# A float32 decoder trunk on one core: bucket transfers in three groups, two tables loaded later, the latents' norm moved into the query's projection

## The chip, the cores and the metric

One NeuronCore of a Trainium2 chip runs the whole program. The metric is the device time of one execution in microseconds. A core has a matrix engine (TensorE, in rows PE), VectorE (DVE), ScalarE (ACT), GpSimd (POOL) and SyncE (SP), which issues nearly all of the DMA transfers here. Each engine runs its own list of instructions in the order of the program and waits on semaphores for the others.

## The reference

A decoder trunk of two layers on 256 tokens of width 1024, all in float32. The first layer has differential attention with a bucketed relative bias; then one shared latent key and value is made; the second layer has multi-head latent attention. Cut to what matters here:

```python
def diff_attention(h, pos, w_qkv, ...):
    qkv = h @ w_qkv
    ...
    bucket = t5_bucket(p_blk[:, :, None] - pos[:, None, :])
    bias = jnp.take(rel_table, bucket, axis=0)
    sc = jnp.where(causal_mask(i, s), sc + bias, NEG_INF)
    a = jax.nn.softmax(sc, axis=-1)
    wts = a[:, :, 0] - lam * a[:, :, 1]
    ...

def shared_latent_kv(h, pos, kv_norm, w_dkv, ...):
    ckv_full = rms_norm(h, kv_norm) @ w_dkv
    c_kv = rms_norm(ckv_full[..., :256], ckv_norm)
    k_pe = rotary(rms_norm(ckv_full[..., 256:], k_pe_norm), pos)
    kv = c_kv @ w_ukv
    ...

def mla_attention(h, pos, w_dq, cq_norm, w_uq, ...):
    c_q = rms_norm(h @ w_dq, cq_norm)
    q = c_q @ w_uq
    ...
```

After each attention come a gated FFN with a causal convolution and a gated per-layer embedding, each with its residual.

## The kernel before, in words

**Weights** come as units of 128 x 1024 words (512 KB), in the order of use. `fetch` (L221 to L230) takes the next of five `st` buffers and has SP issue the transfer. `split_unit` (L235 to L243) makes two halves for a product in three matmuls: ScalarE casts a rounded high part `wh` (L242), and VectorE or GpSimd subtracts it for the low part `wl` (L243, here "lo-split"). Which of the two does it is set by `share`: the fraction of units that goes to GpSimd. `mm3` (L196 to L201) then issues high x high, low x high and high x low; a matmul of 128 columns by 256 is one of these.

**Order.** `weave` and `later` interleave streams as the code is run: attention heads with projections, and a step that is put off by so many units of PE work (`LAG`). A list scheduler then fills each engine's list, by its own estimate of what is ready and in the order of the code otherwise; inside `tc.high_priority()` it prefers an instruction, and `tc.issue_after(x)` keeps one behind instruction x. So the order that comes out is read from the lists (below), not from the code alone. PSUM banks lie in small pools (A 3, T 1, B 2, C 2), so a matmul that takes a bank over waits for the last reader of the old tile.

**First layer.** `proj_a(p)` projects query, key and value of two heads each; `post` squares, norms and transposes them (ACT L341, DVE L342 to L352, GpSimd's power L276 and PE's transposes L193). `bias_prep` (L384 to L437), between the projections, computes the bucket of each distance and writes the 128 x 384 table to device memory (L425, L426). `bias_loads` (L439 to L450) reads it back, broadcast to 32 partitions a piece: 24 transfers of 128 KB into six tiles `oh`. It is put off by `later(LAG, ...)` and issues all 24 at once. `bias_mm` (L452 to L474) compares each tile with the partition's index (DVE L457), does 96 small matmuls for each of three groups with a table of bias values in three parts (PE L464), and has ScalarE write the bias out (L470). Units 12 to 15 are the weights that the projections need next. Attention begins with L529.

**Constants.** `cst` holds gains and small tables; its last part, for the convolution, is loaded after `proj_a` has been queued (L684), and `grow`, two gain rows for the latents, at L862. Both stand in SP's list between the first weight units.

**Between the layers.** With `share` at 0.75 the latent `lps` is projected (320 columns), then `tok_mean` (L301 to L305) sums the squares of the residual by a small matmul with ones (L303), `lat_post` (L985 to L1019) makes the latents' norm and its rotary part (L990 to L1003), and then the query's latent is projected into `dps` (matmuls of 512 columns). `lat_T` transposes the normed latents (PE L193) behind the last of these. `cq_post` norms the query's latent. Then `share` is 0.3, and `fl_b` (L1180) walks `B_ORDER`, a list of items (keys and values, rotary, queries, output projections), woven with the heads of `attn_b`.

## Time and profile before

| what | value |
|---|---|
| median of 3 runs | 789.13 us (787.8 to 789.29) |
| profiled execution | 791.89 us |
| its span | 790.1 us |
| PE busy | 759.5 us, 96%, 6396 matmuls |
| VectorE busy | 560.9 us, 71% |
| ScalarE busy | 486.6 us, 62% |
| GpSimd busy | 278.9 us, 35% |
| mean granted clock of PE | 0.985 |
| read from device memory | 125.75 MB, 161 GB/s over the span |

The profile is of one execution. Its span runs from the first to the last instruction, and 1.8 us of the execution's time lie around it. An engine's busy time is the time in which one of its instructions runs; where an instruction starts late, the row names how long the engine sat idle before it and what released it. [...] Matmuls overlap, so the time of one is read from start to start.

### The profile page before, as it was taken

What the parts mean: (1) busy time and instruction counts of PE and PEld (TensorE: products, weight loads), DVE (VectorE), ACT (ScalarE), POOL (GpSimd) and SP (SyncE); (2) the same over time, 40 slices, a digit from 0 to 9 for tenths busy, and PEclk for the clock granted to TensorE, in tenths of its full rate; (3) what the DMA queues carried; (4) which work ended last, traced back from release to release, by engine and by line L of the source; (5) the groups of instructions that cost most, each with busy time, mean ns of one, the idle gap of its engine ahead of it and who ended that gap; (6) DMA issues with size and microseconds to landing.
All of it is one profiled execution on the core that took longest, in us unless ns stands there. A gap on an engine that the chain in (4) does not pass through costs nothing.

```text
span 790.1 us, 16494 instructions
## 1 busy us (share of the span) xinstructions
PE 759.5 (96%) x6396; PEld 746.0 (94%) x6396; DVE 560.9 (71%) x1137; ACT 486.6 (62%) x1044; POOL 278.9 (35%) x191
## 2 busy tenths in 40 slices
PE   7969999999999999999988999999999999999996
PEld 6969999999999999999978899999999999999996
DVE  6573888658997786546568878866568877875544
ACT  6535887667666665447856777554666666655442
POOL 2653365143233411116735463431333233201221
PEclk9988999999999999999999899999999999999999
DMA  8882345355656576555345132344455556665531
GB/s 317 256 263 92 115 143 166 83 175 154 204 183 185 173 250 207 183 172 172 111 145 183 35 114 71 116 131 130 135 189 172 185 178 186 190 185 186 188 107 54
DMA packets 37519, 127.97 MB, mean 162 GB/s; under 512 B 4672, under 2 KB 6208, under 8 KB 37440
## 3 DMA queue, kind: packets, MB, share of 16 engines
q1 hardware_dynamic: 36720, 126.38, 51.0%
q8 instruction: 50, 0.82, 0.4%
q10 hardware_dynamic: 720, 0.53, 0.2%
q14 instruction: 29, 0.24, 0.1%
HBM read 125.75 MB, written 1.15 MB: 161 GB/s over the span
## 4 chain that ended last, share of the span: by engine, by line
PE 83%; DVE 6%; DMA 3%; ACT 3%; issue 2%; POOL 1%; SPq 1%; DVEq 0%; ACTq 0%; POOLq 0%
PE pa L199 17%; PE pa L201 17%; PE pa L200 17%; PE pc L201 8%; PE pc L200 8%; PE pc L199 8%; DMA st<-in_wall 2%; DVE wl L243 1%; PE pb L529 1%; PE pb L199 1%; PE pt L193 1%; DMA oh<-s 1%; ACT wh L242 1%; POOL wl L243 1%; PE pb L200 1%
## 5 line engine op out<-in xcount | busy, mean ns | idle before, releaser
L242 ACT CAST wh<-st 128x1024 fp32r<-128x1024 f32 x221 | 230.6, 1050 | 171.7 <-PE pa L200 59.1
L243 DVE TENSOR_TENSOR wl<-st,wh 128x1024 fp32r<-128x1024 f32 x156 | 197.9, 1271 | 99.5 <-ACT wh L242 98.3
L243 POOL TENSOR_TENSOR wl<-st,wh 128x1024 fp32r<-128x1024 f32 x65 | 159.8, 2459 | 236.6 <-ACT wh L242 226.7
L201 PE MATMUL pa<-hgH,wl 128*128 128x256 f32 x496 | 141.1, 284 | 0.4 <-POOL wl L243 0.4
L200 PE MATMUL pa<-hgL,wh 128*128 128x256 f32 x496 | 140.5, 283 | 0.0
L199 PE MATMUL pa<-hgH,wh 128*128 128x256 f32 x496 | 140.1, 283 | 0.0
L199 PE MATMUL pa<-wh,hgH 128*128 128x256 f32 x328 | 95.2, 296 | 8.7 <-ACT bias L470 6.0
L199 PE MATMUL pa<-og,wh 128*128 128x256 f32 x352 | 99.9, 287 | 1.4 <-DVE hT L615 1.4
L200 PE MATMUL pa<-og,wh 128*128 128x256 f32 x352 | 99.4, 284 | 0.0
L201 PE MATMUL pa<-og,wl 128*128 128x256 f32 x352 | 99.4, 283 | 0.0
L199 PE MATMUL pc<-hgH,wh 128*128 128x256 f32 x336 | 95.1, 284 | 2.0 <-DVE pa L776 1.4
L201 PE MATMUL pc<-hgH,wl 128*128 128x256 f32 x336 | 95.2, 284 | 1.3 <-DVE wl L243 1.3
L200 PE MATMUL pa<-wl,hgH 128*128 128x256 f32 x328 | 95.0, 291 | 1.5 <-DVE wl L243 0.8
L200 PE MATMUL pc<-hgL,wh 128*128 128x256 f32 x336 | 95.4, 284 | 0.5 <-DVE hgL L209 0.5
L201 PEld LDWEIGHTS pa<-hgH,wl 128*128 128x128 f32 x496 | 95.2, 192 | 0.7 <-POOL wl L243 0.6
L200 PEld LDWEIGHTS pa<-hgL,wh 128*128 128x128 f32 x496 | 95.2, 192 | 0.0
L199 PEld LDWEIGHTS pa<-hgH,wh 128*128 128x128 f32 x496 | 95.1, 192 | 0.1
L201 PE MATMUL pa<-wh,hgL 128*128 128x256 f32 x328 | 94.2, 289 | 0.3 <-DVE hgL L206 0.3
L298 POOL TENSOR_TENSOR ssq<-ssq,d 128x256 f32<-128x256 f32 x35 | 35.9, 1027 | 158.5 <-ACT d L297 158.0
L199 PEld LDWEIGHTS pa<-wh,hgH 128*128 128x128 f32 x328 | 63.8, 197 | 10.9 <-ACT qk L208 6.1
L199 PEld LDWEIGHTS pa<-og,wh 128*128 128x128 f32 x352 | 66.9, 191 | 1.8 <-DVE hT L615 1.6
L200 PEld LDWEIGHTS pa<-og,wh 128*128 128x128 f32 x352 | 67.3, 191 | 0.3
(304 smaller groups left out, 1915.2 us busy)
## 6 DMA issues: line engine op xcount, KB each, us to landing
st<-in_wall SPq DMA_DIRECT2D x225, 512.0 KB, 3.6
oh<-s SPq DMA_DIRECT2D x24, 128.0 KB, 4.0
hT<-in_x SPq DMA_DIRECT2D x4, 256.0 KB, 5.6
st<-in_wall SPq DMA_DIRECT2D x4, 256.0 KB, 5.7
st<-in_xn SPq DMA_DIRECT2D x2, 512.0 KB, 6.5
d<-in_p SPq DMA_DIRECT2D x2, 256.0 KB, 4.7
out_h<-hT SPq DMA_DIRECT2D x4, 128.0 KB, 1.9
out_h<-hT ACTq DMA_DIRECT2D x4, 128.0 KB, 1.9
```

The source lines that it names most:

```text
L193: T.transpose(o, i, ident)
L199: T.matmul(ps, lhsT=aH, rhs=bH, start=start, stop=False)
L200: T.matmul(ps, lhsT=aH, rhs=bL, start=False, stop=False)
L201: lastmm[0] = T.matmul(ps, lhsT=aL, rhs=bH, start=False, stop=stop).ins
L242: A.copy(hi, st)
L243: eng.tensor_sub(lo, st, f(hi))
L298: G.tensor_add(sq, sq, t)
L529: T.matmul(pss[e][:, a:b], lhsT=x[rows, j, t * P:(t + 1) * P], rhs=y[rows, j, :b - a], start=start, stop=stop)
```

## The change

Four things change. The 24 bucket transfers are no longer issued in one go: `fetch` keeps its last transfer in `lastfetch` and calls a hook after units 12, 13 and 14 are issued, and each hook issues the eight transfers of one group behind that unit (`late_loads`). `bias_mm` waits with a group until its tiles are written. The convolution's constants get a hook at unit 18, and `grow` is issued behind whichever unit was issued last. The mean, `epsb` and `lat_post` move into the loop of the query's projection, after its first column block, with priority, behind the last matmul then written. `share` is 0.5 in the latent's stretch in place of 0.75, then 0 until the seventh item of `B_ORDER`, where it becomes 0.3.

```diff
--- before.py
+++ after.py
@@ -81,7 +81,7 @@
 SH_A = 0.5
 SH_FFN = 0.4
 SH_PLE = 0.5
-SH_B0 = 0.75
+SH_B0 = 0.5
 SH_B = 0.3
 
 THRESH = [math.ceil(16.0 * 2.0 ** (3.0 * j / 16.0)) for j in range(1, 16)]
@@ -218,12 +218,16 @@
     turn = [0.0]
     share = [SH_A]
 
+    hooks, lastfetch = {}, [None]
+
     def fetch(pieces=1):
         st = ring.tile([P, UNIT], F32, tag="st", name="st", bufs=BUF_ST)
         u, n = unit_no[0], UNIT // pieces
         unit_no[0] += 1
         for j in range(pieces):
-            nc.sync.dma_start(st[:, j * n:(j + 1) * n], wall[u, :, j * n:(j + 1) * n])
+            lastfetch[0] = nc.sync.dma_start(st[:, j * n:(j + 1) * n], wall[u, :, j * n:(j + 1) * n]).ins
+            if u in hooks:
+                hooks.pop(u)()
             if pieces > 1:
                 yield st
         if pieces == 1:
@@ -425,7 +429,8 @@
         nc.sync.dma_start(s0, bkb[:, :S])
         nc.sync.dma_start(s1, bkb[:, S:])
         bst["pcs"] = []
-        later(LAG, lambda: bias_loads(s0, s1))
+        for n, (kt, half) in enumerate(((0, 0), (0, 1), (1, 0))):
+            hooks[12 + n] = lambda src=(s0, s1)[kt], kt=kt, half=half: bias_loads(src, kt, half)
         bst["tb"], bst["bi"] = tb, bi
         ld = small(2)
         lscr = a_tile()
@@ -436,22 +441,27 @@
         A.activation(le, ld, AF.Exp)
         V.scalar_tensor_tensor(neglam, le[:, 1:2], -LAM_INIT, le[:, 0:1], ALU.add, ALU.subtract)
 
-    def bias_loads(s0, s1):
-        for kt, half in ((0, 0), (0, 1), (1, 0)):
-            nq = 256 if kt == 0 else 128
-            src = s0 if kt == 0 else s1
-            ipp = 2048 // nq
-            for pc in range(2):
-                oh = act.tile([P, ipp, nq], BF16, tag="og", name="oh", bufs=8)
-                i0 = half * 16 + pc * ipp
-                row = src.rearrange("(j i) q -> j i q", i=32)[:, i0:i0 + ipp]
-                for j in range(4):
-                    nc.sync.dma_start(oh[j * 32:(j + 1) * 32], row[j:j + 1].broadcast_to([32, ipp, nq]))
-                bst["pcs"].append(oh)
+    def bias_loads(src, kt, half):
+
+        nq = 256 if kt == 0 else 128
+        ipp = 2048 // nq
+        for pc in range(2):
+            oh = act.tile([P, ipp, nq], BF16, tag="og", name="oh", bufs=8)
+            i0 = half * 16 + pc * ipp
+            row = src.rearrange("(j i) q -> j i q", i=32)[:, i0:i0 + ipp]
+            for j in range(4):
+                late_loads(oh[j * 32:(j + 1) * 32], row[j:j + 1].broadcast_to([32, ipp, nq]))
+            bst["pcs"].append(oh)
+
+    def late_loads(dst, src):
+        with tc.issue_after(lastfetch[0]):
+            nc.sync.dma_start(dst, src)
 
     def bias_mm():
         tb, bi = bst["tb"], bst["bi"]
         for n, (kt, half) in enumerate(((0, 0), (0, 1), (1, 0))):
+            while len(bst["pcs"]) < 2 * n + 2:
+                yield None
             pcs = bst["pcs"][2 * n:2 * n + 2]
             for oh in pcs:
                 V.tensor_scalar(oh, oh, bi, None, ALU.is_equal)
@@ -681,7 +691,7 @@
 
     run(proj_a(0))
     run(proj_a(1))
-    nc.sync.dma_start(cst[:, C_CONV[0]:], consts[:, C_CONV[0]:])
+    hooks[18] = lambda: late_loads(cst[:, C_CONV[0]:], consts[:, C_CONV[0]:])
 
     def ple_p(l):
         pst = d_tile()
@@ -859,7 +869,7 @@
         bigm = bp.tile([P, 384], F32, name="bigm")
         tabs["bigm"] = bigm
         tabs["grow"] = bp.tile([P, 768], F32, name="grow")
-        nc.sync.dma_start(tabs["grow"], grow)
+        late_loads(tabs["grow"], grow)
         G.memset(bigm, 0.0)
         for off in (0, 2 * P):
             v = bigm[:, off:off + P]
@@ -1028,14 +1038,16 @@
         k0 += n
     for n in range(NK):
         split(kvs["hgH"][n // 4][:, n % 4], kvs["hgL"][n // 4][:, n % 4], hT[:, n], col(C_ATTN[1] + n))
-    mx = tok_mean(kvs["sq"])
-    xs["epsb"] = small(NT, "m")
-    V.tensor_scalar(xs["epsb"], mx, EPS, None, ALU.mult)
-    lat_post()
     dps = [bankC() for t in range(NT)]
     for k in range(NK):
         if k % 2 == 0:
             u = load_unit()
+        if k == 1:
+            with tc.high_priority(), tc.issue_after(lastmm[0]):
+                mx = tok_mean(kvs["sq"])
+                xs["epsb"] = small(NT, "m")
+                V.tensor_scalar(xs["epsb"], mx, EPS, None, ALU.mult)
+                lat_post()
         for t in range(NT):
             c = slice((k % 2) * 512, (k % 2 + 1) * 512)
             mm3(dps[t], hH[:, k, t * P:(t + 1) * P], hL[:, k, t * P:(t + 1) * P], u[0][:, c], u[1][:, c], k == 0,
@@ -1043,7 +1055,7 @@
     with tc.issue_after(lastmm[0]):
         bst["lat_T"]()
     cq_post()
-    share[0] = SH_B
+    share[0] = 0.0
 
     nf = [0]
 
@@ -1178,7 +1190,9 @@
     B_ITEMS = {"kv": kv_b, "pe": pe_b, "qn": qn_b, "wo": lambda a: wo(*a)}
 
     def fl_b():
-        for nm, a in B_ORDER:
+        for n, (nm, a) in enumerate(B_ORDER):
+            if n == 6:
+                share[0] = SH_B
             yield from B_ITEMS[nm](a)
 
     weave(attn_b(), fl_b(), RATIO_B)
```

How the order moves, in places. **SP, the weight units and bucket transfers.** Before, SP's list between the first units and the units of the heads (L226 is a weight unit, L449 a bucket transfer, s_532 and s_533 the bucket table, cst and grow the late tables):

```order
L226 DMA st<-in_wall 128x1024 x2
L672 DMA st<-in_xn 128x1024 x2
L684 DMA cst<-in_consts 128x352
L862 DMA grow<-in_grow 128x768
L226 DMA st<-in_wall 128x1024 x6
L425 DMA s_532<-bkb 128x256
L426 DMA s_533<-bkb 128x128
L226 DMA st<-in_wall 128x1024 x2
L449 DMA oh<-s_532 32x2048 x16
L449 DMA oh<-s_533 32x2048 x4
L226 DMA st<-in_wall 128x1024
L449 DMA oh<-s_533 32x2048 x4
L226 DMA st<-in_wall 128x1024 x18
```

Now (L228 is a weight unit; L458 is the line of every late load, a bucket transfer here):

```order
L429 DMA s_532<-bkb 128x256
L228 DMA st<-in_wall 128x1024 x2
L430 DMA s_533<-bkb 128x128
L228 DMA st<-in_wall 128x1024
L458 DMA oh<-s_532 32x2048 x8
L228 DMA st<-in_wall 128x1024
L458 DMA oh<-s_532 32x2048 x8
L228 DMA st<-in_wall 128x1024
L458 DMA oh<-s_533 32x2048 x4
L228 DMA st<-in_wall 128x1024
L458 DMA oh<-s_533 32x2048 x4
L228 DMA st<-in_wall 128x1024 x3
L458 DMA cst<-in_consts 128x352
```

One unit stands ahead of the bucket transfers, and one after each 8, 8 and 4 of them, where 20 stood ahead of unit 12. The tables cst and grow left the place ahead of unit 4; grow is issued 33 units behind cst.

**PE, behind the last matmuls of unit 11** (pa_626 is the projection of units 10 and 11, oh the bucket tiles, tb the table of bias values). Before:

```order
L200 MATMUL pa_626<-wl_636,hgH_120 128x256
L201 MATMUL pa_626<-wh_635,hgL_121 128x256
L193 MATMUL pt_717<-ident_103,d_552 128x128 x4
L464 LDWEIGHTS oh_687
L464 MATMUL pb_733<-tb0_460,oh_687 128x32
```

and, after 96 bias matmuls, unit 12:

```order
L464 LDWEIGHTS oh_692
L464 MATMUL pb_786<-tb2_468,oh_692 128x32
L199 MATMUL pa_1101<-wh_1104,hgH_120 128x256
L200 MATMUL pa_1101<-wl_1105,hgH_120 128x256
L201 MATMUL pa_1101<-wh_1104,hgL_121 128x256
```

Now, at the same place:

```order
L200 MATMUL pa_626<-wl_636,hgH_120 128x256
L201 MATMUL pa_626<-wh_635,hgL_121 128x256
L193 MATMUL pt_687<-ident_103,d_552 128x128 x4
L199 MATMUL pa_700<-wh_713,hgH_120 128x256
L200 MATMUL pa_700<-wl_714,hgH_120 128x256
L201 MATMUL pa_700<-wh_713,hgL_121 128x256
```

and, after the 48 matmuls of units 12 and 13:

```order
L200 MATMUL pa_700<-wl_730,hgH_120 128x256
L201 MATMUL pa_700<-wh_729,hgL_121 128x256
L193 MATMUL pt_781<-ident_103,d_624 128x128 x4
L474 LDWEIGHTS oh_703
L474 MATMUL pb_790<-tb0_460,oh_703 128x32
```

The projection of units 12 and 13 (pa_700, before pa_1101) moved ahead of the first bias group, and so did the transposes of d_624.

**DVE, the compares of the bucket tiles.** Before (oh_702 to oh_712 are the last three of six; wl_1105 is unit 12, wl_1218 unit 14):

```order
L457 TENSOR_SCALAR oh_702<-oh_702,bi_470 128x2048
L209 SCALAR_TENSOR_TENSOR qk_308<-pt_453,cst_83,qk_307 128x512
L346 SCALAR_TENSOR_TENSOR s_546<-s_546,epsx_292 128x8
L457 TENSOR_SCALAR oh_707<-oh_707,bi_470 128x2048
L352 TENSOR_TENSOR d_552<-pa_385,s_550 128x512
L243 TENSOR_TENSOR wl_1105<-st_1102,wh_1104 128x1024
L457 TENSOR_SCALAR oh_712<-oh_712,bi_470 128x2048
L342 TENSOR_REDUCE s_618<-d_617 128x8
L346 SCALAR_TENSOR_TENSOR s_618<-s_618,epsx_292 128x8
L243 TENSOR_TENSOR wl_1218<-st_1215,wh_1217 128x1024
L352 TENSOR_TENSOR d_624<-pa_554,s_622 128x512
```

Now (oh_719 and oh_724 are the second group, oh_1018 and oh_1023 the third; wl_714 is unit 12, wl_1029 unit 14):

```order
L350 SCALAR_TENSOR_TENSOR s_546<-s_546,epsx_292 128x8
L467 TENSOR_SCALAR oh_719<-oh_719,bi_470 128x2048
L467 TENSOR_SCALAR oh_724<-oh_724,bi_470 128x2048
L247 TENSOR_TENSOR wl_714<-st_701,wh_713 128x1024
L356 TENSOR_TENSOR d_552<-pa_385,s_550 128x512
L346 TENSOR_REDUCE s_618<-d_617 128x8
L467 TENSOR_SCALAR oh_1018<-oh_1018,bi_470 128x2048
L350 SCALAR_TENSOR_TENSOR s_618<-s_618,epsx_292 128x8
L467 TENSOR_SCALAR oh_1023<-oh_1023,bi_470 128x2048
L247 TENSOR_TENSOR wl_1029<-st_1016,wh_1028 128x1024
L356 TENSOR_TENSOR d_624<-pa_554,s_622 128x512
```

The compares of the second group stand ahead of unit 12's lo-split, those of the third ahead of unit 14's and of the read-out d_624.

**PE, the end of the query's projection** (pc_5356 and pc_5357, now pc_5318 and pc_5319; L303, now L307, is the mean; ex holds the normed latents, which L193 transposes). Before:

```order
L199 MATMUL pc_5357<-wh_5414,og_5033 128x512
L303 MATMUL pt_5318<-ones_98,ssq_5027 128x2 x2
L200 MATMUL pc_5356<-wl_5415,og_5033 128x512
L201 MATMUL pc_5356<-wh_5414,og_5035 128x512
L200 MATMUL pc_5357<-wl_5415,og_5033 128x512
L201 MATMUL pc_5357<-wh_5414,og_5035 128x512
L199 MATMUL pc_5356<-wh_5414,og_5033 128x512
```

Now:

```order
L200 MATMUL pc_5318<-wl_5415,og_5033 128x512
L201 MATMUL pc_5318<-wh_5414,og_5035 128x512
L199 MATMUL pc_5319<-wh_5414,og_5033 128x512
L200 MATMUL pc_5319<-wl_5415,og_5033 128x512
L307 MATMUL pt_5332<-ones_98,ssq_5027 128x2 x2
L201 MATMUL pc_5319<-wh_5414,og_5035 128x512
L193 MATMUL pt_5430<-ident_103,ex_5350 128x128
L193 MATMUL pt_5430<-ident_103,ex_5360 128x128
```

The mean stood ten matmuls ahead of the end of the projection and stands one ahead of it. Behind the four transposes of ex, two more (the rotary part, into pb_5431) now come ahead of the first projection of keys; before they came later.

## Rows read from the trace of the kernel before

**Rows 1.** The page's first line: span and instructions
```profile
span 790.1 us, 16494 instructions
```

**Rows 2.** Timeline of PE, 46 to 72 us: start, length, line, shapes, count, idle before
```profile
48.86 2.56 PE L464 MATMUL pb<-tb,oh 128*128 128x32 bf16 x96
57.41 0.55 PE L199 MATMUL pa<-wh,hgH 128*128 128x256 f32 x1 [5.99 <-ACT bias L470]
...
65.30 0.28 PE L199 MATMUL pa<-wh,hgH 128*128 128x256 f32 x1
...
65.66 0.28 PE L199 MATMUL pa<-wh,hgH 128*128 128x256 f32 x1
```

**Rows 3.** Busy us by stretch (length, engines, granted clock, DMA share, GB/s)
```profile
40.00:48.00 8.00, 8.00 (x69) 8.00 (x68) 6.01 (x8) 0.69 (x1) 3.00 (x2) 1.00 1.00 242
48.00:53.00 5.00, 3.41 (x105) 3.30 (x104) 2.74 (x4) 2.62 (x4) 1.37 (x1) 1.00 1.02 360
57.50:63.30 5.80, 5.80 (x57) 5.64 (x58) 1.29 (x3) 1.16 (x2) 1.37 (x1) 0.50 0.70 230
70.00:100.00 30.00, 30.00 (x257) 28.25 (x255) 24.09 (x70) 24.04 (x67) 12.42 (x8) 1.00 0.35 107
100.00:137.00 37.00, 36.65 (x311) 35.15 (x309) 31.65 (x89) 29.65 (x82) 20.85 (x13) 1.00 0.52 164
401.20:404.60 3.40, 3.40 (x17) 3.40 (x18) 2.29 (x10) 1.27 (x10) 0.70 (x1) 0.54 0.41 143
420.00:430.00 10.00, 9.74 (x83) 9.50 (x81) 9.16 (x16) 7.37 (x27) 4.50 (x4) 1.00 0.35 119
432.50:439.50 7.00, 6.94 (x35) 6.94 (x35) 3.86 (x16) 3.99 (x14) 1.51 (x2) 0.53 0.29 92
```

**Rows 4.** Timeline of SP (DMA issues), 24 to 52 us
```profile
28.33 12.65 SPq L449 DMA_DIRECT2D oh<-s  x20
41.09 0.38 SPq L226 DMA_DIRECT2D st<-in_wall  x1
```

**Rows 5.** Timeline of ACT, 47 to 58 us
```profile
47.30 1.05 ACT L242 CAST wh<-st 128x1024 fp32r<-128x1024 f32 x1 [8.40 <-DMA st<-in_wall]
48.26 0.59 ACT L341 ACTIVATE d<-pa 128x512 f32<-128x512 f32 x1
```

**Rows 6.** Timeline of DVE, 46 to 58 us
```profile
46.85 0.69 DVE L352 TENSOR_TENSOR d<-pa,s 128x512 f32<-128x512 f32 x1 [1.53 <-POOL s L276]
...
53.35 3.31 DVE L243 TENSOR_TENSOR wl<-st,wh 128x1024 fp32r<-128x1024 f32 x1 [1.80 <-ACT wh L242]
56.58 0.68 DVE L352 TENSOR_TENSOR d<-pa,s 128x512 f32<-128x512 f32 x1
```

**Rows 7.** Timeline of POOL, 47 to 58 us
```profile
53.23 5.65 POOL L243 TENSOR_TENSOR wl<-st,wh 128x1024 fp32r<-128x1024 f32 x2
```

**Rows 8.** Timeline of DVE, 393 to 402.5 us
```profile
398.77 1.22 DVE L243 TENSOR_TENSOR wl<-st,wh 128x1024 fp32r<-128x1024 f32 x1
```

**Rows 9.** Timeline of PE, 393 to 402.5 us
```profile
395.99 0.40 PE L201 MATMUL pc<-wh,og 128*128 128x512 f32 x1
398.42 0.30 PE L193 MATMUL pt<-ident,ex 128*128 128x128 f32 x1 [2.03 <-DVE ex L999]
...
401.17 0.39 PE L201 MATMUL pa<-wh,hgL 128*128 128x256 f32 x1 [0.30 <-DVE hgL L206]
```

**Rows 10.** Timeline of PE, 426 to 434 us
```profile
432.56 1.11 PE L193 MATMUL pt<-ident,d 128*128 128x128 f32 x4 [1.38 <-DVE qk L209]
```

**Rows 11.** Timeline of DVE, 426 to 434 us
```profile
430.08 1.77 DVE L344 TENSOR_SCALAR s<-s 128x4 f32<-128x4 f32 x1
```

**Rows 12.** Timeline of POOL, 426 to 434 us
```profile
429.48 2.35 POOL L243 TENSOR_TENSOR wl<-st,wh 128x1024 fp32r<-128x1024 f32 x1 [2.91 <-ACT wh L242]
```

**Rows 13.** The bucket tile oh, 24 to 70 us: durations ns min/median/max, first and last start
```profile
L457 DVE TENSOR_SCALAR oh<-oh,bi x6: 739/747/753, 36.0 to 50.0; 128x2048 bf16<-128x2048 bf16 x6
```

**Rows 14.** Timeline of PE, 9 to 20.2 us
```profile
19.47 0.39 PE L200 MATMUL pa<-wl,hgH 128*128 128x256 f32 x1 [0.56 <-POOL wl L243]
```

## The prediction

> **What bounds the kernel now.** I read the page first: the span is 790.1 us [rows 1], TensorE (PE) is busy for 96% of it, so a gain can only be idle PE time or PE time at the low clock. The profiled execution took 791.89 us, 0.35% above the median of 789.13 us; I make the sum against the execution and carry the difference over to the median. About 0.2% (1.6 us) is what a measurement of this kernel can tell from no change.
>
> Then the stretches that the diff touches. **Place A** is the bucket-bias load. PE does 96 bias matmuls at 48.86 us and then stands until 57.41 us; the row names 5.99 us of idle, and one line later the clock is the second loss [rows 2]. [...]
>
> Why PE stands: the row blames the bias activation on ScalarE, but that is only the last of several. SP issues 20 bucket transfers in 12.65 us from 28.33 us, and unit 12 only at 41.09 us, behind them [rows 4]. The cast of unit 12 therefore starts at 47.30 us after 8.40 us of idle ScalarE that waits for a transfer [rows 5]. ScalarE keeps the program's order: behind the cast stands the square of the projection bank at 48.26 us. Its norm then goes through VectorE and GpSimd, and VectorE reads the bank out at 56.58 us, behind a lo-split of 3.31 us [rows 6]. That bank is the one which unit 12's matmuls need. The lo-split was slow because GpSimd streamed two of its own at the same time, from 53.23 us [rows 7]; one alone takes 1.22 us [rows 8]. So one late transfer makes the stall.
>
> **Place B** is the latents' norm, and behind it the first heads of the second layer. PE ends the query's projection at 395.99 us, stands 2.03 us for the latents' product and is held up again until 401.17 us [rows 9]; then the clock is 0.54 for 3.4 us [rows 3], 1.6 us lost. Among the first heads PE waits 1.38 us before 432.56 us [rows 10] for an operation that stands behind a VectorE operation on 128x4 elements; that one took 1.77 us [rows 11], beside a lo-split on GpSimd [rows 12]. After that the clock is 0.53 for 7.0 us: 3.3 us lost [rows 3].
>
> **The change, part by part.**
>
> Bucket transfers in three groups. This adds and removes no instruction. On SP unit 12 now precedes all 24 transfers, and units 13, 14 and 15 stand behind the 8th, 16th and 20th. When each lands I estimate from rates: 242 GB/s at a DMA share of 1.00 from 40 to 48 us, mostly buckets, and 360 GB/s from 48 to 53, weights alone [rows 3]. That is 0.53 us for a bucket transfer of 128 KB and 1.4 to 2.1 us for a unit of 512 KB. SP is through with unit 11 at 28.3 us [rows 4]; units 10 and 11 are then still to move. So unit 12 lands at 33 to 35 us, the first eight transfers at 37 to 39, unit 13 at 38 to 41, the next eight at 42 to 45, unit 14 at 44 to 47, four at 46 to 49, unit 15 at 47 to 51, and the last four at 49.5 to 53.5. (Before, the last compare of buckets started at 50.0 us [rows 13].) PE is busy with units 4 to 11 until 48.4 us in either order. Then it has 48 matmuls of units 12 and 13 (0.12 us each: three starts lie between 65.30 and 65.66 us [rows 2]) up to some 54.6 us, 96 bias matmuls of 2.57 us up to 57.5, 19 matmuls, the second 96 from 60, 29 matmuls, and the third 96 from 66. And unit 12's bank is now the one of the projection tile before, which VectorE had read by 46.85 + 0.69 = 47.5 us [rows 6], before PE gets there. So the stall of 6.0 us goes, and with little idle PE I expect no fall of the clock: 6.0 + 2.9 = 8.9 us.
>
> One wait may come in its place. On VectorE the compares of the second group now stand ahead of unit 12's own lo-split: with the transfers there by 45 us and 2 x 0.75 + 1.22 us to do, it ends near 47.7, just before PE asks for it. The two compares of the third group stand ahead of a lo-split (unit 14's) and of the read-out whose result PE transposes at 54.6 us, before the first bias matmuls. With the last transfer at 51.5 us, the middle of my estimate, the compare is through at 52.3 (0.75 us [rows 13]), the split, partly beside GpSimd, near 54.3 and the read-out (0.68 us [rows 6]) at 55.0: PE waits about 0.5 us; nothing if the transfer lands before 51.
>
> What is late next: the heads. They start at about 70 us in either case, with 8.9 us less PE work behind them. From 70 to 137 us VectorE was busy 24.09 + 31.65 = 55.7 of 67 us and ScalarE 53.7 [rows 3]. Eight us less leave 59; some 5 us of VectorE's work (lo-splits and evacuations of units that PE then has behind it) move ahead of 70 us, so 51 of 59, 86%. Tight but not full; I take 1 us back, since PE stood for only 0.35 us in all of the 67 us before. The ends are 0, and 4: half an us at each of eight heads, about a third of the 1.38 us that a head of the second layer cost [rows 10]. **A: -8.9 + 0.5 + 1 = -7.4 us (-8.9 to -4.4).**
>
> Late constants. They leave the full DMA stretch before unit 4, which lands some 2 us earlier. But PE's last stop there, 0.56 us, was on a lo-split that GpSimd was slow at [rows 14]; from 19.47 us PE has no stop until the bias matmuls. I count 0 (0 to -0.6). Behind the 19th unit, or for the wider table still later, their 180 + 393 KB (128 x 352 and 128 x 768 words) cost 2.4 us of DMA where its share is 0.35 to 0.52 [rows 3]. If that cover went, a unit would come 2.4 us late, at most once.
>
> The latents' norm. By the words it moves into the query's projection, with priority. The order of PE says otherwise: the small matmul of the mean, until now 10 matmuls before the end, stands one matmul before the end. So it is not earlier. Walked by hand: mean at 396.2 us, VectorE to 396.9, GpSimd's power to 397.9. The next lo-split on VectorE now stands ahead of the product, and its cast waits for the projection's end at 396.4 us [rows 9] and takes 1.05, as the cast in [rows 5], so it runs 397.5 to 398.75; the product, which stood ahead of it (the split then ran at 398.77 us [rows 8]), comes 1 us later. Also two transposes of the rotary part now stand ahead of the first projection of keys. PE resumes full work near 402.1 us, where it was 401.17. **+1 us (0 to +3**; 3 if the longer idle doubles the clock loss of 1.6 us).
>
> GpSimd's share of lo-splits, 0 until the seventh item of the second layer's list. In the first heads GpSimd has two lo-splits in place of three, and at other units; 12 matmuls of filler (12 x 0.12 = 1.4 us) move between the scores and the next transposes. I still find four small stops there, together 2 to 3 us, about the old sum. What I expect to go is half of the clock's 3.3 us: **-1.7 us (-3.3 to +1.7**, the worse end being one more stop like the 1.38 us and its tail). GpSimd does 4 lo-splits fewer in all, VectorE 4 more: 4 x 1.22 = 4.9 us, beside PE work as long as VectorE has room.
>
> [...]
>
> From 440 us on the order differs again, with equal PE work; 0 (-2 to +2). The FFN stretches are the same. **Sum: -7.4 + 1 - 1.7 = -8.1 us**, 783.8 us for the profiled execution, 781.0 us for the median.
>
> **Rivals.**
> 1. The heads give half of A back: with PE's backlog gone, VectorE at 86% and ScalarE as full, each of eight heads leaves PE half a us idle. A is then -4.4, the sum -5.1: 784.0 us. For it speaks how close the two engines stand; against it that PE stood for only 0.35 us there before. If the squeeze is full, nothing of A stays, and the time is 788.
> 2. Slower: VectorE becomes the bound between 400 and 440 us, since with share 0 all lo-splits queue there. Price: 4.9 us of splits, a longer half-clock tail of 3.3 us, B's +1, and no gain of 1.7, against A's 7.4: +1.8, or 790.9 us. It decides if VectorE has no gaps left there; it was busy 9.16 of 10 us before 430 [rows 3]. Against it: the 1.77-us operation was slow through GpSimd [rows 11, 12], and that goes away.
> 3. The third part does what it says: the chain hides, PE loses neither 2.03 us nor the clock's 1.6 after it: -3.6 in place of +1, so 776.4 us. Against it stands the order of PE.
> 4. The transfers set the time, not their order: the same 5.2 MB in the same full stretch. If the last bucket lands at 53.5 us or later and the split behind its compare runs beside GpSimd for 3.31 us, PE's transposes come at 58 us: a stop of 3.4 us, and, if the clock falls again, 2.9 more. A is -1.6, the sum -2.3: 786.8 us. [...]
>
> **How the numbers follow.** My forecast 0.48, rival 1 0.18, rival 2 0.09, rival 3 0.11, rival 4 0.14. The likely ends of the forecast's terms, about 3 us either way, give 778 to 784.5. The range takes in rivals 1, 3 and 4 and leaves out rival 2 and the full squeeze of 1: 776 to 787. Faster by over 0.2%: all but rival 2 and 0.05 of rivals 1 and 4, 0.86. Within 0.2%: that 0.05 and 0.01 of rival 2, 0.06. Slower: the rest of rival 2, 0.08.
>
> **What would show it.** Right: PE stops of no more than 1 us between 48 and 70 us, granted clock 1.0 there, the cast of unit 12 before 40 us, the first head still near 70 us; the mean's matmul at the projection's very end, with PE idle of about 3 us behind it. Wrong: PE stops that name VectorE among the eight heads (rival 1), transposes at 55 us or later behind a compare of buckets (4), or a clock under 0.6 for over 7 us between 400 and 440 (2).

## The result: slower by half a per cent

The changed kernel takes **792.71 us** (median of 5 runs, 790.02 to 796.46), the kernel before 788.83 us beside it (5 runs, 787.17 to 789.29). The ratio is 1.0055, 95% interval 1.0028 to 1.0082: slower by more than the 0.2% that can be told from no change. The forecast was 781.0 us, faster.

The profiled execution of the changed kernel took 794.3 us. Its page (first line; busy us of PE and VectorE; granted clock, the share of TensorE's full clock as the profile gives it, in tenths, in 40 slices of 19.8 us) answers to [rows 1]:

```profile
span 792.5 us, 16464 instructions
...
PE 766.0 (97%) x6396; PEld 751.3 (95%) x6396; DVE 565.3 (71%) x1141; ACT 485.8 (61%) x1044; POOL 271.7 (34%) x187
...
PEclk9999997999999999999989899999999999999999
```

PE does the same 6396 matmuls and is busy 97% of a longer span: it is busy longer at the same work, and the clock line says where: the 7 in the seventh slice, 119 to 139 us. That is in the heads of the first layer, some sixty us behind the bias matmuls.

The forecast's own place first. The waits of PE from 40 to 160 us in the changed kernel (engine, tile and line, what it waited for; total, times, longest):

```profile
PE pt L193 <- DVE d L356: 3.1, 1, 3.1
PE pa L199 <- ACT og L208: 1.9, 2, 1.0
PE pc L193 <- DVE qk L209: 0.9, 1, 0.9
```

The stop of 5.99 us on the bias activation [rows 2] is gone, as forecast. A stop of 3.1 us is new, before the transposes; and so are three stops of about 1 us among the heads. The first, in the timelines of SP, ScalarE, VectorE, GpSimd and PE (start, length, engine, line, shapes, count, idle before):

```profile
28.27 0.33 SPq L228 DMA_DIRECT2D st<-in_wall  x1
28.65 4.33 SPq L458 DMA_DIRECT2D oh<-s  x8
33.09 0.36 SPq L228 DMA_DIRECT2D st<-in_wall  x1
...
43.66 3.81 SPq L458 DMA_DIRECT2D oh<-s  x4
```
```profile
40.89 1.05 ACT L246 CAST wh<-st 128x1024 fp32r<-128x1024 f32 x1 [2.68 <-issue]
```
```profile
53.32 2.06 DVE L467 TENSOR_SCALAR oh<-oh,bi 128x2048 bf16<-128x2048 bf16 x1 [3.69 <-DMA oh<-s]
55.30 1.21 DVE L247 TENSOR_TENSOR wl<-st,wh 128x1024 fp32r<-128x1024 f32 x1
56.44 0.68 DVE L356 TENSOR_TENSOR d<-pa,s 128x512 f32<-128x512 f32 x1
```
```profile
52.45 2.38 POOL L247 TENSOR_TENSOR wl<-st,wh 128x1024 fp32r<-128x1024 f32 x1 [1.09 <-ACT wh L246]
```
```profile
53.92 0.28 PE L201 MATMUL pa<-wh,hgL 128*128 128x256 f32 x1
57.26 1.09 PE L193 MATMUL pt<-ident,d 128*128 128x128 f32 x4 [3.06 <-DVE d L356]
58.14 2.71 PE L474 MATMUL pb<-tb,oh 128*128 128x32 bf16 x96
...
73.68 0.95 PE L539 MATMUL pb<-qk 64*128 64x128 f32 x6
```

Unit 12 is issued at 28.27 us instead of 41.09 [rows 4], and its cast, at 40.89 us instead of 47.30 [rows 5], names no transfer that it waits for. The last four bucket transfers are issued by 47.5 us and the compare that needs them starts at 53.32, after 3.69 us in which VectorE waits for the transfer. The compare runs beside GpSimd's split and takes 2.06 us instead of 0.75 [rows 13]; behind it stand the split and the read-out that PE transposes. The last row is the first head: 73.68 us, where the kernel before has it at 69.68:

```profile
69.68 0.95 PE L529 MATMUL pb<-qk 64*128 64x128 f32 x6
```

The stretches of the changed kernel (length, busy us of the engines, granted clock, DMA share, GB/s), to be read against [rows 3]:

```profile
40.00:48.00 8.00, 8.00 (x69) 8.00 (x68) 6.86 (x10) 3.64 (x4) 4.90 (x3) 1.00 1.01 259
...
53.00:57.30 4.30, 1.24 (x11) 1.06 (x11) 3.98 (x4) 0.32 (x1) 1.83 (x1) 0.93 0.57 225
57.50:63.30 5.80, 5.80 (x129) 5.69 (x129) 4.78 (x6) 4.76 (x13) 2.19 (x1) 0.78 0.75 250
74.00:100.00 26.00, 26.00 (x200) 23.21 (x199) 19.37 (x63) 18.34 (x56) 9.05 (x6) 0.95 0.34 102
...
112.00:122.00 10.00, 7.24 (x55) 6.13 (x53) 7.77 (x20) 7.62 (x25) 7.74 (x4) 0.98 0.43 158
122.00:133.00 11.00, 11.00 (x58) 10.45 (x59) 7.25 (x31) 6.93 (x26) 1.39 (x2) 0.56 0.17 49
```

Behind 57.5 us the clock is 0.78 instead of 0.50. With the length of a stretch times what its clock lacks to 1.00 as an estimate of the loss, that is 1.3 us of 5.8 instead of 2.9: more than half is gone too. But from 112 to 122 us PE stands for 2.8 us, and then has 11 us at 0.56: 4.8 us more, by the same estimate. In the same part of the heads (100 to 137 us) PE stood 0.35 us before, at a clock of 1.00 [rows 3].

**Where the time went.** I set both traces side by side at points where PE has done equal work: each matmul counted at the median distance from its start to the next for its form, and what passes beyond that is time lost to an idle PE or a low clock. Us lost, by stretch of PE's work (work 40 is at 48 us, 60 at 72 to 79, 120 at 138 to 144, 372 at the latents, 400 to 420 the first heads of the second layer); 'before, again' is a second profile of the kernel before (789.7 us, below):

```
work             0-40  40-60  60-120  120-372  372-400  400-420  420-740   all
before            8.4   10.2    -0.1      2.3      5.6      8.2      6.4  41.0
before, again     8.8    9.7    -0.1      2.3      5.5      6.2      6.4  38.8
changed           7.8    4.0    11.7      2.6      6.8      6.8      3.5  43.1
```

The bias stretch (40 to 60) gains 5.7 us, the heads (60 to 120) lose 11.8, and what is left over all stretches, 4.3 us against 'before, again', is the result (4.6 us between the two executions). It is all there at the first mean behind the heads, which comes 4.9 us later (table below).

### The profile page after: what moved, and what is told of

Same layout as the page of the kernel before. It is cut to its first block, busy times and chain, and to the rows that moved or that the text cites. A ratio compares the mean times of both kernels' runs of the same rounds, so it can differ in the third digit from the quotient of the medians.

```text
span 792.5 us, 16464 instructions
## 1 busy us (share of the span) xinstructions
PE 766.0 (97%) x6396; PEld 751.3 (95%) x6396; DVE 565.3 (71%) x1141; ACT 485.8 (61%) x1044; POOL 271.7 (34%) x187
## 4 chain that ended last, share of the span: by engine, by line
PE 82%; DVE 5%; DMA 4%; ACT 3%; POOL 3%; issue 1%; SPq 0%; POOLq 0%; DVEq 0%; ACTq 0%
PE pa L199 17%; PE pa L200 17%; PE pa L201 17%; PE pc L201 8%; PE pc L200 8%; PE pc L199 8%; DMA oh<-s 2%; POOL wl L247 2%; DMA st<-in_wall 2%; ACT wh L246 1%; DVE wl L247 1%; PE pb L539 1%; PE pc L193 1%; PE pt L193 1%; PE pb L474 1%
## 5 line engine op out<-in xcount | busy, mean ns | idle before, releaser
L247 DVE TENSOR_TENSOR wl<-st,wh 128x1024 fp32r<-128x1024 f32 x160 | 204.9, 1282 | 94.4 <-ACT wh L246 85.5
L247 POOL TENSOR_TENSOR wl<-st,wh 128x1024 fp32r<-128x1024 f32 x61 | 150.5, 2467 | 225.4 <-ACT wh L246 216.7
```

What stands on the lines that cost most here:

```text
L247: eng.tensor_sub(lo, st, f(hi))
```

## Experiments

**Theory H.** The heads of the first layer set the end of their stretch. Each is a chain through VectorE and ScalarE, and PE is busy beside them only because matmuls of units 12 to 15 and later are left to put between ("filler"). Whatever the order puts ahead of the first head delays that head, and is missing behind it. PE's order has 36 matmuls of units from 12 on ahead of the first head before, and 110 in the changed kernel, since in the order of the code each bias group now stands behind the unit that releases its transfers. The rivals are named in each expectation.

### The parts alone

Three runs split the change, and one takes the groups out of it.

```diff
# e1_old_groups, against the changed kernel
-        for n, (kt, half) in enumerate(((0, 0), (0, 1), (1, 0))):
-            hooks[12 + n] = lambda src=(s0, s1)[kt], kt=kt, half=half: bias_loads(src, kt, half)
+        later(LAG, lambda: bias_loads(s0, s1))
...
-            while len(bst["pcs"]) < 2 * n + 2:
-                yield None
```

> The change with the bucket transfers as they were before (all 24 in one go), the late tables, the norm's place and the shares as changed. Theory H (the heads of the first layer set the end of their stretch, and the groups start them 4 us later; the other parts gain some 2.7 us): the first head starts within 1 us of 69.7 us, the first layer's mean is within 1 us of 167.5 us, and the time is 785 to 787 us, 5 to 7 under the change. Rival V (VectorE bound by the shares of the second layer, my rival 2): the time stays at 791 us or more. Rival L (the loss comes from the late tables): the mean stays near 172 us.

Measured: 781.52 us (780.13 to 786.98), ratio to before 0.9929 (0.9902 to 0.9957). The change without its main part is faster than before by 7 us: the groups cost 11 us in this company. Rivals V and L fall. H has the direction, but all its numbers are missed: the first head comes at 63.2 us and the mean at 161.5, 6 us earlier than it wanted, and the time lies below its range. The late tables, to which H gave nothing, move them, as the run of the tables alone shows below.

```diff
# e2_groups_only, against the kernel before
+        for n, (kt, half) in enumerate(((0, 0), (0, 1), (1, 0))):
+            hooks[12 + n] = lambda src=(s0, s1)[kt], kt=kt, half=half: bias_loads(src, kt, half)
...
+            while len(bst["pcs"]) < 2 * n + 2:
+                yield None
```

> Before, with the three groups alone: tables, norm and shares as before. Theory H: first head near 73.7 us, mean of the first layer near 172.4 us, and 793 to 795 us, 4 to 6 over before. Rivals V and L: within 2 us of before, since neither the second layer nor the tables are touched.

Measured: 793.59 us (791.96 to 797.91), ratio 1.009 (1.0063 to 1.0117), a time as H wants. The 3.1-us stop is not among its waits: PE loses 0.2 us in work 40 to 60 (and 2.2 us more than 'before, again' ahead of that, 1.6 us of it in one stop). So the 3.1-us stop is not needed for a loss in the heads: 6.8 us go there, in stops like the changed kernel's. But the mean, which H wanted near 172.4 us, comes at 167.0, no later than in 'before, again' (167.5): here the stop that is gone pays for the heads. The 2.3 us by which this execution, the run's fastest, is longer lie behind the first layer, and where the rest of the 5.1 us between the medians lies no profile shows. A stretch of this run's heads:

```profile
110.00:120.00 10.00, 8.17 (x54) 7.25 (x53) 7.78 (x21) 7.64 (x25) 7.64 (x4) 0.83 0.45 158
```

```diff
# e3_norm_share_only, against the kernel before
-SH_B0 = 0.75
+SH_B0 = 0.5
...
+        if k == 1:
+            with tc.high_priority(), tc.issue_after(lastmm[0]):
+                mx = tok_mean(kvs["sq"])
...
-    share[0] = SH_B
+    share[0] = 0.0
...
+            if n == 6:
+                share[0] = SH_B
```

> Before, with the norm's place and the shares changed, transfers and tables as before. Theory H: 2 to 3 us under before (786 to 787), PE's stop at the latents some 1 us longer than the 2.03 us of before, and less lost among the first heads of the second layer. Rival V: 2 us or more over before.

Measured: 787.23 us (783.68 to 789.62, 12 runs), ratio 0.9984 (0.9965 to 1.0002). About 1 us gained, no more than can be told from none, and less than H's 2 to 3; in the first heads of the second layer PE loses 5.4 us instead of 6.2 to 8.2.

```diff
# e4_tables_only, against the kernel before
-    nc.sync.dma_start(cst[:, C_CONV[0]:], consts[:, C_CONV[0]:])
+    hooks[18] = lambda: late_loads(cst[:, C_CONV[0]:], consts[:, C_CONV[0]:])
...
-        nc.sync.dma_start(tabs["grow"], grow)
+        late_loads(tabs["grow"], grow)
```

> Before, with the two tables loaded late and nothing else. Theory H: within 1 us of before (788 to 789), as PE's start of the span is bound by the lo-splits. Rival L: 2 us or more over before.

Measured: **777.19 us** (775.45 to 779.48), ratio 0.9867 (0.9844 to 0.9889). A miss of 11 us, of the prediction too, which had put this part at nothing; and the fastest kernel of the study. SP and ScalarE in its trace:

```profile
26.88 13.61 SPq L453 DMA_DIRECT2D oh<-s  x24
40.80 12.04 SPq L228 DMA_DIRECT2D st<-in_wall  x7
```
```profile
42.50 0.60 ACT L345 ACTIVATE d<-pa 128x512 f32<-128x512 f32 x1 [4.27 <-DVE s L346]
45.65 1.05 ACT L246 CAST wh<-st 128x1024 fp32r<-128x1024 f32 x1 [2.55 <-DMA st<-in_wall]
```

With two tables out of SP's way the bucket transfers start at 26.88 us instead of 28.33 [rows 4], and unit 12's cast at 45.65 instead of 47.30 [rows 5]: 1.7 us. What counts more is the other difference: the square of the projection bank (42.50) now stands ahead of that cast, where it stood behind it at 48.26 [rows 5]. The norm's chain no longer waits for unit 12. The longest wait of PE from 40 to 160 us in this run is this one; the stop of 6 us is gone:

```profile
PE pc L201 <- DVE wl L247: 0.6, 1, 0.6
```

Its first head comes at 60.9 us.

The parts add up to +5.1 - 11.3 - 1.2 = -7.4 us, and together they give +3.9: the groups and the tables remove the same stop, so that gain is not had twice, while the groups' loss in the heads stays.

### Why so small a part gains so much

```diff
# e6_square_first, against the kernel before: unit 12's cast kept behind the square
-        A.copy(hi, st)
+        if unit_no[0] == 13 and lastsq[0] is not None:
+            with tc.issue_after(lastsq[0]):
+                A.copy(hi, st)
+        else:
+            A.copy(hi, st)
...
-                A.activation(s2[:, i * z:(i + 1) * z], p, AF.Square)
+                lastsq[0] = A.activation(s2[:, i * z:(i + 1) * z], p, AF.Square).ins
```

> Before, with one instruction moved: ScalarE's cast of unit 12 is kept behind the square of the projection bank that it stood ahead of. PE's order is that of before, tables and transfers too. Theory S (late tables helped only by that order on ScalarE): PE's stop of 6.0 us at 51 us falls below 2 us, the first head starts near 62 to 64 us, and the time is 779 to 783 us. Rival T (it is the landing of the transfers, 1.6 us earlier): the stop stays above 4 us and the time within 2 us of before.

Measured: 785.8 us (783.49 to 788.33, 12 runs), ratio 0.9968 (0.9955 to 0.9982). The edit moves no transfer, PE's order is that of before, and the stop shrinks to 1.1 us:

```profile
PE pa L199 <- DVE d L358: 1.1, 1, 1.1
```

The first head comes at 62.7 us. So this one edit takes most of the stop away, as theory S says; the time gained, 2.7 us between the medians, is smaller than it says. Two more things differ, though. ScalarE and VectorE of this run:

```profile
42.95 0.60 ACT L347 ACTIVATE d<-pa 128x512 f32<-128x512 f32 x1 [4.54 <-DVE s L348]
45.08 1.05 ACT L246 CAST wh<-st 128x1024 fp32r<-128x1024 f32 x1 [1.54 <-DMA st<-in_wall]
```
```profile
51.12 0.69 DVE L358 TENSOR_TENSOR d<-pa,s 128x512 f32<-128x512 f32 x1 [1.53 <-POOL s L282]
51.73 2.78 DVE L249 TENSOR_TENSOR wl<-st,wh 128x1024 fp32r<-128x1024 f32 x1
```

VectorE's list changed with the pair, in five places: the norm's reduction now stands ahead of unit 12's lo-split, and the read-out ahead of the next one, where they stood behind [rows 6]. (The lists of PE, SP and GpSimd are those of before.) And unit 12 is cast at 45.08 us, 2.2 us earlier than before [rows 5], because its transfer landed earlier in this execution. An estimate can part the two. With the old order the read-out came 8.8 to 9.3 us behind unit 12's cast (47.30 to 56.58 [rows 5, 6]; 47.65 to 56.44 in 'before, again'; 46.73 to 55.74 in norm and shares alone). Behind a cast at 45.08 that makes 53.9 to 54.4 us; measured is 51.12. So some 3 us of the stop are the order, and some 2 us can be rival T's earlier landing, which this run does not exclude. In the run of the tables alone the read-out came at 50.17 us, where its cast at 45.65 makes 54.4 to 54.9: 4 to 5 us by the order.

In the table of lost time work 40 to 60 falls from 9.7 to 3.7 us, the heads stay at -0.1, and the second layer stays as it was (8.3 us in its first heads). Most of the rest of the tables' 11 us lies there, where the order with late tables differs from before: that run loses 3.2 instead of 6.2 to 8.2 us in the first heads, 3.0 instead of 6.4 behind them. PE's waits in the first heads of the second layer, 'before, again' from 425 to 455 us and tables alone from 395 to 452 us:

```profile
PE pt L193 <- DVE qk L209: 1.4, 1, 1.4
PE pc L193 <- DVE dr L206: 1.1, 1, 1.1
PE pt L193 <- DVE sa L1133: 1.0, 1, 1.0
PE pb L199 <- ACT qk L208: 0.8, 1, 0.8
```
```profile
PE pb L201 <- DVE qk L209: 0.8, 1, 0.8
PE pb L199 <- ACT qk L208: 0.8, 1, 0.8
```

Why moving two transfers made the order there another one stays open; no run separates it.

### More or less work ahead of the first head

```diff
# e5_tables_gate, against e4: the bias groups wait until unit 13 is issued
+        while unit_no[0] < 14:
+            yield None
```

> Experiment 4 (late tables alone) with one thing more: the stream of bias and heads may not begin until unit 13 has been asked for, so that 86 filler matmuls stand ahead of the first head on PE in place of 33. Nothing is added or removed. Theory H (the heads' own chain sets the end of the first layer's stretch, 98 us after the first head): first head 53 x 0.12 = 6.4 us later, near 67 us, the first mean near 165 to 166, and the time 782 to 785 us. Rival F (PE's total work sets it, and filler done early is filler saved later): first mean within 1.5 us of 159.2, time 776 to 779.

Measured: 789.6 us (787.99 to 792.36, 12 runs), ratio 1.0019 (1.0006 to 1.0032), 12.4 us above the run it differs from. Rival F (PE's total work sets the end) falls: the mean comes at 167.2 us, not near 159.2. H has the direction, and its time was too small by 5 us: 86 matmuls ahead of the first head instead of 33, 6.5 us lost in the heads instead of 0.0, and the second layer's order changed again (6.9 instead of 3.2 in its first heads), which H does not speak of. So about half of the 12.4 us lies in the heads of the first layer.

```diff
# e7_groups_early (10) and e10_hooks13 (13), each against the changed kernel
-            hooks[12 + n] = lambda src=(s0, s1)[kt], kt=kt, half=half: bias_loads(src, kt, half)
+            hooks[10 + n] = lambda src=(s0, s1)[kt], kt=kt, half=half: bias_loads(src, kt, half)
...
+            hooks[13 + n] = lambda src=(s0, s1)[kt], kt=kt, half=half: bias_loads(src, kt, half)
```

> The change, with the three groups behind units 10, 11 and 12 in place of 12, 13 and 14: 67 filler matmuls stand ahead of the first head on PE, where the change has some 110. Theory H: if PE has no stop, the first head starts near 65 us, the mean near 163 to 164 and the time is 783 to 786 us. Rival F: within 2 us of the change (791 to 795).

> The changed kernel with its three groups one unit later (behind the 13th, 14th and 15th unit), which puts 119 filler matmuls ahead of the first head in place of 110 (groups one unit earlier: 67, and 783.7 us). Theory H (what is put ahead of the first head is missing behind it): first head at 74 to 76 us, first mean of the heads at 172 to 175, time 792 to 797. Rival D (the changed kernel loses only by its own stop at 54 us, and any other place is better): first mean below 170, time 785 to 790.

Measured: groups two units earlier 783.71 us (781.71 to 785.17), ratio 0.9941 (0.9923 to 0.9959); one unit later 793.16 us (790.25 to 793.97), ratio 1.0054 (1.0031 to 1.0078). The first has a stop of 2.3 us at the transposes and one of 1.1, about as much as the changed kernel, and is 9 us faster, so the stop is not what makes the change slow. The second has its first mean at 172.2 us, where D wanted it below 170; H's three numbers are met. All profiled executions in order of the matmuls ahead of the first head (times in us; 'lost' is the table's work 60 to 120; 'mean' is the first product with `ones` behind the heads, L303 before; 'clock' is the mean granted clock from the head to the mean):

```
                     matmuls  first head  lost   mean   mean - head   clock
tables alone              33        60.9   0.0  159.2          98.3    1.00
without the groups        33        63.2  -0.1  161.5          98.3    1.00
square first              36        62.7  -0.1  160.6          97.9    1.00
before, again             36        69.5  -0.1  167.5          98.0    1.00
groups 2 units earlier    67        69.7   2.5  164.7          95.0    1.00
tables, gate              86        70.8   6.5  167.2          96.4    1.00
groups alone             110        73.1   6.8  167.0          93.9    0.98
changed                  110        73.7  11.7  172.4          98.7    0.93
groups 1 unit later      119        75.8  11.2  172.2          96.3    0.96
```

The stretch from the first head to the mean takes 94 to 99 us in all of them, though up to 86 matmuls (of 0.12 us [rows 2], 10 us) fewer stand in it. Nothing is lost there with 33 or 36 ahead: PE's own work fills the stretch. From 67 on some is lost, in no strict order (6.5 us with 86). What differs between 'groups alone' and 'changed' with the same 110 (6.8 and 11.7) is the clock. It stood at 0.50 for 13.6 us in the heads of the changed kernel and for 3.4 us in those of the groups alone, first two stretches, then one:

```profile
97.60:101.00 3.40, 3.40 (x15) 3.15 (x15) 1.81 (x4) 0.94 (x3) 0.63 (x1) 0.50 0.22 88
121.50:131.70 10.20, 10.20 (x50) 9.38 (x49) 6.45 (x28) 6.30 (x23) 1.39 (x2) 0.50 0.18 53
```
```profile
113.50:116.90 3.40, 3.40 (x15) 3.18 (x16) 3.00 (x13) 1.81 (x6) 1.77 (x2) 0.50 0.92 335
```

If half of that time is lost, an estimate, it makes 6.8 and 1.7 us (half is the upper end for a matmul of 128x256: at 0.50 it starts 0.21 us behind the one before, at 98.73 and 98.94 us of the changed kernel, at 1.00 0.12 us [rows 2]); without it both lose about 5 us in the heads, and both stretches take 92 us from head to mean. Why the clock fell twice in the one and once in the other stays open. So H holds in part: matmuls moved ahead of the heads delay them and are missing behind them, for about 5 us with 110, and in the changed kernel the clock costs up to 6.8 us more, by that estimate.

### Shares and norm apart

```diff
# e8_tables_share: e4 and the shares alone
-SH_B0 = 0.75
+SH_B0 = 0.5
...
-    share[0] = SH_B
+    share[0] = 0.0
...
+            if n == 6:
+                share[0] = SH_B
```
```diff
# e9_tables_norm: e4 and the norm's new place alone
+        if k == 1:
+            with tc.high_priority(), tc.issue_after(lastmm[0]):
+                mx = tok_mean(kvs["sq"])
...
```

> Experiment 4 (late tables alone) with the changed shares, the norm where it was. It tells which of the two parts made experiment 1 slower than experiment 4 by 4.3 us. Theory H (the later norm costs about 1 us, the shares gain 1 to 2): 775 to 777 us. Rival V (the shares load VectorE): 780 us or more.

> Late tables (as in the run of the tables alone, 777.2 us) and the latents' norm inside the query's projection, with the shares of filler as in the kernel before. The run of the tables and the shares took 780.6, that of tables, norm and shares 781.5. Theory V (the shares cost about 3 us, the norm about 1): 777 to 779. Rival W (norm and shares cost alike, or only together): 779.5 to 782.

Measured: tables and shares 780.55 us (779.82 to 781.68), ratio 0.9903 (0.9886 to 0.992); tables and norm 778.69 (777.46 to 783.99), ratio 0.9892 (0.9865 to 0.992). With the late tables the shares cost 3.4 us (no run of the one overlaps the other's), though with the old ones they cost none: the waits of the first heads become, from 395 to 452 us,

```profile
PE pa L199 <- DVE d L356: 2.1, 1, 2.1
PE pb L199 <- DVE s L348: 0.9, 1, 0.9
```

the same two as in the changed kernel and in norm and shares alone. With the shares the first heads lose 5.4 us, whichever way the tables are loaded (e3, e8); without them 3.2 with late tables and 6.2 to 8.2 with the old. H's 775 to 777 is missed; that VectorE's load is the reason, as V has it, is not shown. For the norm the figure agrees with V, but the intervals of the two runs overlap, and between 777.2 and 778.7 no difference is shown. Where the mean stands tells more. PE at the latents, first of the changed kernel, then of tables and shares, then of tables and norm:

```profile
400.82 0.50 PE L307 MATMUL pt<-ones,ssq 128*128 128x2 f32 x4
...
404.54 0.30 PE L193 MATMUL pt<-ident,ex 128*128 128x128 f32 x1 [2.88 <-DVE ex L1009]
```
```profile
389.36 0.50 PE L307 MATMUL pt<-ones,ssq 128*128 128x2 f32 x4
...
393.08 0.30 PE L193 MATMUL pt<-ident,ex 128*128 128x128 f32 x1 [2.88 <-DVE ex L1007]
```
```profile
386.60 0.50 PE L307 MATMUL pt<-ones,ssq 128*128 128x2 f32 x4
...
391.56 0.30 PE L193 MATMUL pt<-ident,ex 128*128 128x128 f32 x1 [2.03 <-DVE ex L1007]
```

With the shares and without the norm's move the mean stands one matmul ahead of the projection's end, as in the changed kernel, and the stop is 2.88 us. With the move and without the shares the mean stands ten ahead, as before, and the stop is the old 2.03 [rows 9]. So the shares make it longer by 0.85 us, and the move leaves it as it is.

### The kernel before, profiled again

No edit.

> The kernel before, unchanged, profiled once more, since its one profile was of its slowest execution. If what the prediction read there is the kernel's own: the stop before L193 at 51 us 5 to 7 us long, first head at 68 to 70 us, first mean of the heads at 166 to 168. If it was that execution's: the stop under 3 us and the first head at 62 to 65. Time 787 to 790 in either case.

Measured: 789.7 us. Its stop, with the same first head (69.5 us) and mean (167.5):

```profile
PE pa L199 <- DVE d L352: 5.5, 1, 5.5
```

So the stop that the prediction read is the kernel's own. In the first heads of the second layer this execution lost 2.0 us less than the first one, with the same program: that much of what was read there was one execution's.

## Why the prediction was wrong

**The stop and its clock (-8.9, with 0.5 back): right in kind, too large.** The stop on the bias activation is gone; unit 12 is cast at 40.89 us, 0.9 behind the 40 us given, and no longer waits for its transfer; the clock behind is 0.78. The stretch gained 5.7 us, not 8.4. No run shows the 2.9 us of clock in the 8.9 as such: shown are 5.8 us at a clock of 0.50 [rows 3], of which 2.9 is half, and in them a matmul of 128x256 starts 0.21 us behind the one before (57.76 and 57.97 us) where it is 0.12 at 1.00 [rows 2], which would make 2.5 us. What is missing is rival 4's stop: the last bucket's compare at 53.32 us where that rival has its transfer at 53.5 or later, and 3.1 us of idle PE where it has 3.4. The slow operation was the compare (2.06 us) and not the split behind it (1.21). The new order did bring unit 12 forward, but the last compare went back from 50.00 us [rows 13] to 53.32. The "PE waits about 0.5 us" was mis-sized by 2.6 us, since the transfer was set in the middle of an estimate (51.5 us) whose late end (53.5) came true.

**The heads (+1, 0 to +4): the step that failed.** They lost 11.8 us. "They start at about 70 us in either case" is the smaller miss. The prediction's own count (48, 19 and 29 matmuls between the bias groups; 14 more follow) leads there, since these matmuls take the place of the old stop; the new stop and the clock of 0.78 behind it make it 73.7. What the step had wrong is the stretch behind the first head. It summed VectorE's work ("tight but not full", 51 of 59 us) and took nearly all of the 8.9 us of missing PE work for a gain, which makes 90 us up to the mean in place of 98; and it gave the clock there no term at all. Measured are 98.7 us. Each head is a chain, and with 74 matmuls fewer beside it PE stood for 2.8 us in three stops; the clock of 0.50 cost 6.8 us, by the estimate above; the remaining 2.2 us are rows in which PE is busy and slow. Without the clock the stretch is 92 us, in the groups alone too: 6 of the 8.9 us would have been gained. Rival 1 names stops in the heads, but for another reason. Only one of the three names VectorE, which was busy for 19.37 of 26 us and 7.77 of 10, so not full; and it ends at 788 us even in full.

**Late constants (0): wrong where they stand alone, without effect in the whole.** Alone they gain 11.3 us. The prediction counted the transfers' time, found cover for it and stopped, when it had written itself that ScalarE keeps the program's order and that the square stands behind the cast. It did not ask whether a change in SP's list would turn that pair. Run e6, which turns it, has 1.1 us left of the stop, but gains 2.7 us and not 11: the order is some 3 us of the stop, and most of the tables' other gain lies in the second layer, for a reason that no run shows.

**Latents' norm (+1): right in size, wrong in cause.** The stretch loses 1.3 us more (6.8 against 5.5), 0.85 of it in the stop before the transposes. That the mean is not earlier was right; but the later mean and the longer stop come with the shares (e8) and not with the norm's move (e9). The rest of the 1.3 has no clear owner: the stretch lost 5.1 us in e9 and 6.3 in e4, with the same stop.

**Shares (-1.7): right alone, not in company.** With the old tables the first heads lose 0.8 to 2.8 us less in e3; with the late ones 2.2 more in e8. In the whole change they lose 6.8, between the two profiles of before (6.2 and 8.2). Rival 2 falls: from the latents through these heads the changed kernel loses 13.6 us, the two profiles of before 13.8 and 11.7.

**From work 420 on (0, -2 to +2):** 2.9 us gained, a little outside. Rival 3 falls with the norm. In sum over the stretches, against 'before, again', -1.0 - 5.7 + 11.8 + 0.3 + 1.3 + 0.6 - 2.9 = +4.4 us (4.3 unrounded), against -8.1.

## What to carry to other kernels

Idle time that is removed from an engine is not gained if the work that fills it is missing later: find the first link of the chain behind it (here the first head) in the new order, count what now stands ahead of it, ask what will cover the chain once that work is used up, and give the clock there a term too. Where the long wait is one instruction queued behind another on an engine in program order, turning the two is the cheap repair; here that alone gained 2.7 us. Two constant loads moved out of a full stretch (a DMA share of 1.02 from 10 to 16 us before), which turned the same pair and more of the order far behind it, gained 11 us, and that kernel, the late tables alone at 777.2 us, beats both. Two parts of a change that remove the same stop are not to be added up, and each is to be tried alone.

## What was unexpected of the hardware

The clock fell behind a stretch in which PE's rows show no idle time. From 98 to 100 us the changed kernel's PE is busy all of the time by its rows and has a granted clock of 0.50:

```profile
95.00:98.00 3.00, 3.00 (x15) 2.07 (x15) 2.68 (x8) 1.36 (x4) 1.84 (x2) 0.94 0.43 134
98.00:100.00 2.00, 2.00 (x9) 1.78 (x9) 1.41 (x3) 0.21 (x1) 0.23 (x1) 0.50 0.15 61
```

Before it stand 3 us with 15 matmuls, where the stretch from 74 to 100 us has 23 in 3 us on average. A busy PE in these rows is thus no sign that it works at its pace, and the count of its instructions says more. And a compare of 128x2048 bf16, 0.75 us in all six of the kernel before [rows 13], took 2.06 us beside a split on GpSimd, nearly three times as long; another of the changed kernel's six, at 37.82 us, took 2.84 us beside one from 37.70. That is no mark of the groups: with the tables alone two of the six, at 32.49 and 38.13 us, took 2.50 and 2.54 us, also beside splits on GpSimd. Nor is an operation always slow there: the changed kernel's lo-split on VectorE at 45.15 us took 1.22 us, with one on GpSimd from 45.24.
